# Two neighbouring chunks change places in every second channel tile of an RWKV-7 stage

## The chip, the cores and the metric

The kernel runs on one core of a Trainium2 chip. The core has a matrix engine (TensorE, in the profile PE, with its weight loads as PEld), VectorE (DVE), ScalarE (ACT), GpSimd (POOL), a queue engine (SP) and 16 DMA engines. Each engine takes its own instructions in order and waits for the others by semaphores. SBUF is the working memory with 128 partitions; PSUM receives what TensorE computes, in banks of 512 fp32 values a partition. The metric is the device time of one execution in microseconds, and lower is better.

## The reference

One decoder layer over 1024 tokens of 1024 channels. After an RMSNorm and one input projection, an RWKV-7 mixer of 8 heads of 64 channels and a sparse attention run in parallel; their outputs are gated, merged and projected, and a SwiGLU network and a last norm follow. The part that the change touches is the recurrence:

```python
def step(state, inp):
    r_t, d_t, k_t, v_t, kk_t, a_t = inp
    sa = jnp.einsum('bhij,bhj->bhi', state, -kk_t)
    state = (state * d_t[:, :, None, :] + sa[..., None] * (kk_t * a_t)[:, :, None, :]
             + v_t[..., None] * k_t[:, :, None, :])
    return state, jnp.einsum('bhij,bhj->bhi', state, r_t)
```

Then y is normalized for each head, scaled and shifted, a bonus is added and the sum is multiplied by a gate.

## The kernel before

**Halves, quarters, pairs, chunks.** The 1024 tokens are handled as two halves of 512. `rwkv(half, ...)` goes through two quarters of 256 tokens each (q = 0 to 3 over the whole run), a quarter has two pairs `pr`, a pair two chunks of 64 tokens, `pa` = 0 and 1. The 512 channels of the mixer are four channel tiles `ct` of 128 partitions, so two heads share a channel tile: head h is in tile h // 2, in its upper or lower 64 partitions.

**What comes ahead of a chunk.** The projections of the mixer (`proj_rwkv`, before the stage) write each channel tile with its 1024 tokens to DRAM, one DMA from a staging tile of which there are two (L307). A quarter loads its 256 tokens (L528), computes decays and gates (L547 to L566), norms (L593 to L612), the products of keys and queries for each chunk (L667, masked into MT at L671), their transposes (L686 into NAT), and inverts triangular 64x64 blocks: a chain of 62 small VectorE instructions (L705, L707) on 32x32 blocks, whose result goes through DRAM into TT (L709, L718), is transposed to TZ (L721), and is completed on TensorE (L735, L756).

**Positions.** In the tiles of a pair, chunk pa = 0 has its corrected values in partitions 64 to 127 (`ba` = 64 - 64 pa) and its plain values in 0 to 63 (`kb` = 64 pa); chunk pa = 1 the other way round. So TT, rhs and UV hold both chunks side by side in the partitions.

**A step of a chunk** is a chain across three engines (L783 to L817): matmuls of the state with AR (L788, eight heads); on VectorE, the result is added to `rhs` (L794), and on ScalarE the other half is copied to y2 (L795); eight matmuls with TT (L800), where all heads use the 64 rows and 64 output partitions at `ba`; a copy with a minus sign to UV (L802); eight matmuls with NAT (L810); and two VectorE instructions that make the new state (L813, L814). Behind each pair come the outputs of both chunks (L821), the inner products of the next pair (L745), and a norm. `finish` (L762) transposes, scales, adds the bonus and multiplies by the gate; that of the first pair stands in the last chunk's step.

**Filler.** The order on TensorE is written out by hand. `fill` is a queue of generators with matmuls of other stages: projections, attention of half 0, the merge and the first part of the feed-forward network. `pump(n)` emits about n matmuls of it at the place where it is called, in pieces that are mostly of four; `ticks(n, m)` emits n in m pieces, and steps the selection of the attention in between (`beside`). So each link of the chain has a number of filler matmuls behind it: in half 0 these are 6, 6 and 7, in half 1 they are 8, 8 and 9. Between the triangular inversion's start and L735 stand 251, 236, 281 and 241 in the four quarters. The order on the other engines is made by a scheduler from the program, with its own costs and priorities.

**Weights.** Filler tiles take weights of 512 KB through three staging buffers, split into two parts by L114 on ScalarE and L115 on VectorE; three products of the parts stand for one fp32 matmul (L140, L141, L145).

Of the kernel before, what the change touches and what calls it, by code (L numbers as in the profile page):

```python
# [18 lines left out]
AF = mybir.ActivationFunctionType  # L19
ALU = mybir.AluOpType  # L20
# [14 lines left out]
CT_R, CT_K, CT_V, CT_WA, CT_GD = 0, 4, 8, 12, 13  # L35
# [6 lines left out]
P_N1, P_N2, P_NF, P_MU, P_W0, P_A0, P_KK, P_KA, P_LG, P_LB, P_RK = 0, 8, 16, 24, 38, 42, 46, 50, 54, 58, 62  # L42
# [7 lines left out]
def block_kernel(ctx: ExitStack, tc: tile.TileContext, ins: dict, outT: bass.AP, stop=None, dbg=None):  # L50
    nc = tc.nc
    V, A, G, T, SY = nc.vector, nc.scalar, nc.gpsimd, nc.tensor, nc.sync
# [10 lines left out]
    par = cp.tile([128, NPAR], F32, name="par")  # L63
# [8 lines left out]
    hb = cp.tile([128, 16], F32, name="hb")  # L72
# [217 lines left out]
    def shifted(st, half, ct, x):  # L290
# [226 lines left out]
    def rwkv(half, p, consts, ready=None):  # L517
# [5 lines left out]
        for q in range(2 * half, 2 * half + 2):  # L523
# [17 lines left out]
            for c in range(2):  # L541
                pss = [mix(), mix()]
                for e in range(2):
                    ct = 2 * c + e
                    for i, ps in enumerate(pss):
                        half_ = slice(64 * i, 64 * i + 64)
                        T.matmul(ps[:, e * 256:(e + 1) * 256], wup[half_, ct * 128:(ct + 1) * 128], wa[half_, :],  # L547
                                 start=True, stop=True)
                for i, t in enumerate((L, ta)):
                    for ct in (2 * c, 2 * c + 1):  # L550
                        A.activation(t[:, ct, :], pss[i][:, ct % 2 * 256:ct % 2 * 256 + 256], AF.Tanh, scale=0.5,
                                     bias=hb[:, 4 * i + ct:4 * i + ct + 1])
# [6 lines left out]
            P = p.tile([128, 4, 4, 65], F32, tag="P", name="P")  # L559
# [27 lines left out]
            ps = sums(sq)  # L587
# [3 lines left out]
            ps = mix()  # L591
# [170 lines left out]
            def finish(pr, yc, y2):  # L762
                pt = mix()
                pg = mix()
                yT = y2.rearrange("p (c t) -> p c t", c=4)
                for ct in range(4):
                    T.transpose(pt[:, ct * 128:(ct + 1) * 128], yc[:, ct * 128:(ct + 1) * 128], ident)
                    T.matmul(pg[:, ct * 128:(ct + 1) * 128], gup[:, ct * 128:(ct + 1) * 128],
                             sg[:, pr * 128:(pr + 1) * 128], start=True, stop=True)
                for ct in range(4):  # L770
                    A.activation(yT[:, ct, :], pt[:, ct * 128:(ct + 1) * 128], AF.Identity,
                                 scale=par[:, P_LG + ct:P_LG + ct + 1], bias=par[:, P_LB + ct:P_LB + ct + 1])
# [6 lines left out]
            for pr in range(2):  # L779
                yb = p.tile([128, 2, 512], F32, tag=("P", "x6")[pr], name="yb")  # L780
                yc, y2 = yb[:, 0, :], yb[:, 1, :]
                for pa in range(2):
                    c = 2 * pr + pa  # L783
                    ba, kb = 64 - 64 * pa, 64 * pa
                    st = sref[0]
                    as_ = [mix(), mix()]
                    for h, ct, ro, hc in hd:
                        T.matmul(as_[h % 2][:, ct * 64:ct * 64 + 64],  # L788
                                 AR[ro, ct, c, :, :].rearrange("p s t -> p (s t)"), st[ro, ct, :],
                                 start=True, stop=True)  # L790
                    for g in range(2):
                        a4 = as_[g][:, 0:256].rearrange("p (c t) -> p c t", c=4)
                        r4 = rhs.rearrange("p (c g t) -> p c g t", c=4, g=2)[ba:ba + 64, :, g, :]
                        V.tensor_tensor(r4, a4[ba:ba + 64], r4, op=ALU.add)  # L794
                        A.activation(y2.rearrange("p (c g t) -> p c g t", c=4, g=2)[kb:kb + 64, :, g, :],  # L795
                                     a4[kb:kb + 64], AF.Copy)
                    pump(6 if half == 0 else 8)
                    ps = mix()
                    for h, ct, ro, hc in hd:
                        T.matmul(ps[ba:ba + 64, hc], TT[ba:ba + 64, pr, h, :], rhs[ba:ba + 64, hc],  # L800
                                 start=True, stop=True)
                    A.activation(UV[pr][ba:ba + 64, pa, :], ps[ba:ba + 64, :], AF.Copy, scale=-1.0)  # L802
                    if late and pa == 1:
                        finish(*late)
                        late = None
                    else:
                        pump(6 if half == 0 else 8)
                    ps = mix()
                    for h, ct, ro, hc in hd:
                        T.matmul(ps[ro, ct * 64:ct * 64 + 64], NAT[pr][:, pa, hc], UV[pr][:, pa, hc],  # L810
                                 start=True, stop=True)
                    new = cp.tile([128, 4, 64], F32, tag="S", name="S", bufs=2)
                    V.tensor_tensor(new, ps[:, 0:256].rearrange("p (c t) -> p c t", c=4), st, op=ALU.add)  # L813
                    V.tensor_tensor(new, new, PC[:, :, c:c + 1].to_broadcast([128, 4, 64]), op=ALU.mult)  # L814
# [677 lines left out]
```

## Time and profile before

| | |
|---|---|
| runs | 1746.47, 1748.87, 1750.44 us (median 1748.87) |
| profiled execution | 1748.71 us |
| its span, first to last instruction | 1746.9 us |
| TensorE busy | 1708.1 us (98%) |
| VectorE busy | 1114.3 us (64%) |
| ScalarE busy | 833.3 us (48%) |
| DMA | 247.14 MB, mean 141 GB/s |

The profile has a page with busy times, a span cut into slices, DMA queues, the chain that ended last, and the costliest groups of instructions. Further views list groups by line and form, the instructions in order of time, waits, and busy times of given stretches. A group's row reads: line, engine, operation, output<-inputs, rows*columns of the array and shape, count | busy us, mean ns of one | idle time before it, and what ended that. In the order of time, a row begins with start and duration in us from the span's start. A matmul in fp32 is two passes, and each pass has a record of its own; the end of a pass is modelled.

### The profile page before, as it was taken

Reading aid. Unit: us, or ns where it says so; the run is one execution under the profiler, and the core shown is the slowest. Engines: PE = TensorE matmul, PEld = TensorE weight load, DVE = VectorE, ACT = ScalarE, POOL = GpSimd, SP = SyncE. Lnnn points to the kernel's source line nnn. Section 1 sums busy time; section 2 is a strip of 40 time slices with the busy share of each in tenths; the row PEclk is TensorE's granted clock in tenths of the full one; section 3 lists DMA queues with packets and bytes.
Section 4 is the critical chain, followed back from the end, with each engine's and each line's share of the span. In section 5 each row is a group of like instructions: output and inputs, shape, how many; then the busy total and the mean of one; then the engine's idle time right before and its main releaser. Section 6 shows DMA issues by size and latency. Waiting matters only on the chain.

```text
span 1746.9 us, 26692 instructions
## 1 busy us (share of the span) xinstructions
PE 1708.1 (98%) x10156; PEld 1410.3 (81%) x10156; DVE 1114.3 (64%) x2133; ACT 833.3 (48%) x1547; POOL 100.5 (6%) x123
## 2 busy tenths in 40 slices
PE   8999999999999998999999999999999999999997
PEld 6888888778878776878787888888788888888887
DVE  6789899857468567857876655445465564454464
ACT  6365998453445687645333455433234322232241
POOL 0000000010021111000100321000000000000000
PEclk9999999999999999999999999999999999999999
DMA  5542224536357535644343765173464344434442
GB/s 210 173 138 94 97 97 145 163 97 171 100 178 201 149 121 157 197 146 118 97 127 93 234 165 138 61 225 113 165 213 140 109 136 151 136 96 150 139 124 93
DMA packets 132383, 247.14 MB, mean 141 GB/s; under 512 B 36848, under 2 KB 60080, under 8 KB 132128
## 3 DMA queue, kind: packets, MB, share of 16 engines
q1 hardware_dynamic: 108896, 171.61, 31.7%
q10 hardware_dynamic: 15552, 47.75, 8.7%
q0 software_dynamic: 7808, 26.09, 5.6%
q8 instruction: 80, 1.31, 0.3%
q14 instruction: 47, 0.39, 0.1%
HBM read 192.40 MB, written 53.00 MB: 140 GB/s over the span
## 4 chain that ended last, share of the span: by engine, by line
PE 50%; issue 1%; DVE 1%; ACT 0%; POOLq 0%; POOL 0%; DVEq 0%; ACTq 0%
PE acc L145 14%; PE acc L140 13%; PE acc L141 13%; PE acc L156 3%; PE mix L1053 1%; PE mix L1029 1%; PE mix L1043 1%; PE acc L1197 0%; PE mix L800 0%; PE mix L788 0%; PE acc L1201 0%; ACT whi L114 0%; DVE h L1272 0%; PE mix L254 0%; PE mix L810 0%
## 5 line engine op out<-in xcount | busy, mean ns | idle before, releaser
L115 DVE TENSOR_TENSOR wlo<-wst,whi 128x1024 fp32r<-128x1024 f32 (+1 forms) x229 | 277.5, 1214 | 276.0 <-PE acc L145 132.7
L114 ACT ACTIVATE whi<-wst 128x1024 fp32r<-128x1024 f32 (+1 forms) x229 | 238.3, 1043 | 262.7 <-PE acc L141 186.9
L140 PE MATMUL acc<-zhi,whi 128*128 128x512 f32 x672 | 264.8, 394 | 0.0
L141 PE MATMUL acc<-zlo,whi 128*128 128x512 f32 x672 | 262.0, 390 | 0.0
L145 PE MATMUL acc<-zhi,wlo 128*128 128x512 f32 x672 | 170.2, 392 | 0.0
L140 PEld LDWEIGHTS acc<-zhi,whi 128*128 128x128 f32 x672 | 126.2, 188 | 26.8 <-issue 1.9
L141 PEld LDWEIGHTS acc<-zlo,whi 128*128 128x128 f32 x672 | 126.3, 188 | 24.8
L145 PEld LDWEIGHTS acc<-zhi,wlo 128*128 128x128 f32 x672 | 124.8, 188 | 25.4 <-issue 0.7
L140 PE MATMUL acc<-u1hi,whi 128*128 128x512 f32 x352 | 140.5, 399 | 0.1
L141 PE MATMUL acc<-u1lo,whi 128*128 128x512 f32 x352 | 137.6, 391 | 0.0
L140 PE MATMUL acc<-u0hi,whi 128*128 128x512 f32 (+1 forms) x352 | 135.5, 387 | 1.7 <-DVE tmp L323 1.7
L141 PE MATMUL acc<-u0lo,whi 128*128 128x512 f32 (+1 forms) x352 | 133.8, 383 | 0.0
L140 PE MATMUL acc<-fhi,whi 128*128 128x512 f32 (+1 forms) x318 | 114.3, 368 | 2.3 <-ACT whi L114 1.5
L141 PE MATMUL acc<-flo,whi 128*128 128x512 f32 (+1 forms) x318 | 112.9, 364 | 0.2 <-DVE flo L115 0.2
L145 PE MATMUL acc<-u1hi,wlo 128*128 128x512 f32 x352 | 90.0, 394 | 0.0
L145 PE MATMUL acc<-u0hi,wlo 128*128 128x512 f32 (+1 forms) x352 | 85.7, 384 | 0.0
L114 ACT ACTIVATE fhi<-tmp 128x512 fp32r<-128x512 f32 x44 | 27.7, 630 | 112.6 <-DVE tmp L1229 112.3
L140 PEld LDWEIGHTS acc<-u0hi,whi 128*128 128x128 f32 x352 | 66.2, 188 | 14.9 <-ACT stg L114 2.1
L140 PEld LDWEIGHTS acc<-u1hi,whi 128*128 128x128 f32 x352 | 66.2, 188 | 14.8 <-issue 1.3
L141 PEld LDWEIGHTS acc<-u1lo,whi 128*128 128x128 f32 x352 | 66.2, 188 | 12.6
L141 PEld LDWEIGHTS acc<-u0lo,whi 128*128 128x128 f32 x352 | 66.2, 188 | 12.1
L145 PEld LDWEIGHTS acc<-u1hi,wlo 128*128 128x128 f32 x352 | 64.9, 188 | 13.7 <-issue 0.9
(328 smaller groups left out, 3204.2 us busy)
## 6 DMA issues: line engine op xcount, KB each, us to landing
wst<-in_w_ffn_in SPq DMA_DIRECT2D x72, 512.0 KB, 3.6
wst<-in_w_in ACTq DMA_DIRECT2D x36, 512.0 KB, 4.5
wst<-in_w_in SPq DMA_DIRECT2D x27, 512.0 KB, 4.0
wst<-in_w_fo SPq DMA_DIRECT2D x25, 512.0 KB, 3.8
k<-d_k POOLq DMA_DIRECT2D x24, 512.0 KB, 7.9
h<-in_xT SPq DMA_DIRECT2D x32, 256.0 KB, 5.2
d_g<-tmp ACTq DMA_DIRECT2D x32, 256.0 KB, 3.4
tmp<-d_g SPq DMA_DIRECT2D x32, 256.0 KB, 3.7
```

Source lines behind the costliest of these rows:

```text
L114: A.activation(hi, x, AF.Copy)
L115: V.tensor_tensor(lo, x, hi.bitcast(F32), op=ALU.subtract)
L140: T.matmul(ps, whi[:, wk + k, :], ahi[:, ak + k, tok], start=k == 0, stop=False)
L141: T.matmul(ps, whi[:, wk + k, :], alo[:, ak + k, tok], start=False, stop=False)
L145: T.matmul(ps, wlo[:, wk + k, :], ahi[:, ak + k, tok], start=False, stop=k == nk - 1)
L156: T.matmul(ps, w[:, k, :], a[:, k, tok], start=k == 0 and w is whi and a is ahi, stop=k == nk - 1 and a is alo)
L1029: T.matmul(ps[:, :w], q[bi // 2][:, e, bi % 2 * 128:bi % 2 * 128 + 128], k[:, i, e, c:c + w], start=i == 0, stop=i == 1)
L1043: T.transpose(ps[:, j * 128:(j + 1) * 128], L[:, (c + j) * 128:(c + j + 1) * 128], ident)
L1053: T.matmul(py[64 * e:64 * e + 64, bi * 128:(bi + 1) * 128], v[:, j, 64 * e:64 * e + 64], pts[e][j // 4][:, j % 4, :], start=j == b, stop=j ...
```

## The change

In odd channel tiles the two chunks of each pair change places. The swap is made on the way: where the projections of r, k and v write odd channel tiles to DRAM, two DMAs with pieces of 64 tokens write each pair's two chunks into each other's place; the tanh of decay and gate inputs writes odd tiles in two pieces; the decays at the chunks' ends (PC) are copied in three instructions. In a step, `at[x]` gives for even (x = 0) and odd (x = 1) channel tiles the position and the partitions of the chunk in hand, and the instructions over all four tiles become one for even and one for odd tiles: four adds and four copies for two and two, two copies to UV for one. The TT matmuls go through the heads in the order 0, 2, 1, 3, 4, 6, 5, 7, and take their partitions by tile. `finish` swaps back, with two ScalarE instructions for each odd tile and three adds for one.

With it, the filler behind the links of a step is 8, 8 and 9 matmuls in both halves, and that ahead of L735 in quarter 0 is 211.

```diff
+    def swapped(x):
+        return x.rearrange("p (n s t) -> p n s t", s=2, t=64)
...
-                SY.dma_start(d_rw[g0][j], st.rearrange("p h t -> p (h t)"))
+                if g0 in (CT_R, CT_K, CT_V) and j % 2:
+                    d, t = (swapped(x) for x in (d_rw[g0][j], st.rearrange("p h t -> p (h t)")))
+                    for i in range(2):
+                        SY.dma_start(d[:, :, i, :], t[:, :, 1 - i, :])
+                else:
+                    SY.dma_start(d_rw[g0][j], st.rearrange("p h t -> p (h t)"))
...
+                        xy = [(x, y)] if ct % 2 == 0 else [(swapped(x)[:, :, j, :], swapped(y)[:, :, 1 - j, :])
+                                                           for j in range(2)]
...
-            V.tensor_copy(PC, P[:, :, :, 64])
+            V.tensor_copy(PC[:, 0::2, :], P[:, 0::2, :, 64])
+            for i in range(2):
+                V.tensor_copy(PC[:, 1::2, i::2], P[:, 1::2, 1 - i::2, 64])
...
-            ticks((251, 236, 281, 241)[q], (13, 4, 10, 6)[q])
+            ticks((211, 236, 281, 241)[q], (13, 4, 10, 6)[q])
...
-                V.tensor_tensor(yT, yT, bon[:, :, pr * 128:(pr + 1) * 128], op=ALU.add)
+                b = bon[:, :, pr * 128:(pr + 1) * 128]
+                V.tensor_tensor(yT[:, 0::2, :], yT[:, 0::2, :], b[:, 0::2, :], op=ALU.add)
+                for i in range(2):
+                    y = yT[:, 1::2, 64 * i:64 * i + 64]
+                    V.tensor_tensor(y, y, b[:, 1::2, 64 - 64 * i:128 - 64 * i], op=ALU.add)
...
-                    ba, kb = 64 - 64 * pa, 64 * pa
+                    at = [(pa ^ x, 64 - 64 * (pa ^ x), 64 * (pa ^ x)) for x in range(2)]
...
-                        r4 = rhs.rearrange("p (c g t) -> p c g t", c=4, g=2)[ba:ba + 64, :, g, :]
-                        V.tensor_tensor(r4, a4[ba:ba + 64], r4, op=ALU.add)
-                        A.activation(y2.rearrange("p (c g t) -> p c g t", c=4, g=2)[kb:kb + 64, :, g, :],
-                                     a4[kb:kb + 64], AF.Copy)
-                    pump(6 if half == 0 else 8)
+                        for x, (pp, ba, kb) in enumerate(at):
+                            r4 = rhs.rearrange("p (c g t) -> p c g t", c=4, g=2)[ba:ba + 64, x::2, g, :]
+                            V.tensor_tensor(r4, tiles(x, as_[g][ba:ba + 64, 0:256]), r4, op=ALU.add)
+                    for g in range(2):
+                        for x, (pp, ba, kb) in enumerate(at):
+                            A.activation(y2.rearrange("p (c g t) -> p c g t", c=4, g=2)[kb:kb + 64, x::2, g, :],
+                                         tiles(x, as_[g][kb:kb + 64, 0:256]), AF.Copy)
+                    pump(8)
                     ps = mix()
-                    for h, ct, ro, hc in hd:
+                    for h, ct, ro, hc in (hd[i] for i in (0, 2, 1, 3, 4, 6, 5, 7)):
+                        ba = at[ct % 2][1]
                         T.matmul(ps[ba:ba + 64, hc], TT[ba:ba + 64, pr, h, :], rhs[ba:ba + 64, hc],
                                  start=True, stop=True)
-                    A.activation(UV[pr][ba:ba + 64, pa, :], ps[ba:ba + 64, :], AF.Copy, scale=-1.0)
+                    for x, (pp, ba, kb) in enumerate(at):
+                        A.activation(tiles(x, UV[pr][ba:ba + 64, pp, :]), tiles(x, ps[ba:ba + 64, :]), AF.Copy, scale=-1.0)
...
-                        pump(6 if half == 0 else 8)
+                        pump(8)
...
-                        pump(7 if half == 0 else 9)
+                        pump(9)
```

More of the change, by code (lines that the diff above doesn't have):

```diff
@@ L770, in finish @@
                 for ct in range(4):
-                    A.activation(yT[:, ct, :], pt[:, ct * 128:(ct + 1) * 128], AF.Identity,
-                                 scale=par[:, P_LG + ct:P_LG + ct + 1], bias=par[:, P_LB + ct:P_LB + ct + 1])
-                V.tensor_tensor(yT, yT, bon[:, :, pr * 128:(pr + 1) * 128], op=ALU.add)
+                    x, y = pt[:, ct * 128:(ct + 1) * 128], yT[:, ct, :]
+                    xy = [(x, y)] if ct % 2 == 0 else [(x[:, 64 - 64 * i:128 - 64 * i], y[:, 64 * i:64 * i + 64])
+                                                       for i in range(2)]
+                    for x, y in xy:
+                        A.activation(y, x, AF.Identity, scale=par[:, P_LG + ct:P_LG + ct + 1],
+                                     bias=par[:, P_LB + ct:P_LB + ct + 1])
+                b = bon[:, :, pr * 128:(pr + 1) * 128]
[3 more added lines that the diff above has]
+                    V.tensor_tensor(y, y, b[:, 1::2, 64 - 64 * i:128 - 64 * i], op=ALU.add)
                 V.tensor_tensor(yT, yT, pg.rearrange("p (c t) -> p c t", c=4), op=ALU.mult)
@@ L806, in rwkv @@
                     else:
-                        pump(6 if half == 0 else 8)
+                        pump(8)
                     ps = mix()
                     for h, ct, ro, hc in hd:
-                        T.matmul(ps[ro, ct * 64:ct * 64 + 64], NAT[pr][:, pa, hc], UV[pr][:, pa, hc],
+                        pp = at[ct % 2][0]
+                        T.matmul(ps[ro, ct * 64:ct * 64 + 64], NAT[pr][:, pp, hc], UV[pr][:, pp, hc],
                                  start=True, stop=True)
```

10 lines of the change are left out of this document (6 added, 4 removed).

## The prediction

> **What bounds the kernel now.** First the page: busy times, then stretches of time, then groups by form.
>
> ```profile
> PE 1708.1 (98%) x10156; PEld 1410.3 (81%) x10156; DVE 1114.3 (64%) x2133; ACT 833.3 (48%) x1547; POOL 100.5 (6%) x123
> ...
> 350.00:393.00 43.00, 41.01 (x264) 32.93 (x263) 25.46 (x46) 22.51 (x53) 4.52 (x2) 1.00 0.38 99
> 393.00:437.00 44.00, 44.00 (x198) 36.49 (x198) 30.97 (x81) 16.03 (x28) 0.77 (x1) 1.00 0.60 172
> 480.00:620.00 140.00, 137.13 (x1099) 109.86 (x1097) 93.45 (x225) 79.35 (x171) 26.14 (x32) 1.00 0.60 176
> 620.00:800.00 180.00, 171.00 (x1335) 136.97 (x1334) 123.14 (x257) 124.41 (x271) 10.55 (x6) 0.98 0.49 150
> 800.00:960.00 160.00, 156.25 (x1142) 127.19 (x1141) 118.37 (x226) 59.75 (x98) 10.09 (x5) 1.00 0.37 110
> ```
>
> A row of stretches reads: stretch, length, then busy time and count of PE, PEld, DVE, ACT, POOL, granted clock, DMA share, GB/s. The RWKV stage (the first to the last of its lines) lies between about 345 and 955 us, and even there PE is busy for 95% or more: every wait is covered by filler matmuls of other stages. The total of filler is fixed, so the time is the sum of what TensorE issues plus the few gaps. An edit is worth what it takes off that sum, unless it opens a gap. (A busy row is modelled with a tail, so I work below with distances from start to start.) The groups by form, RWKV lines only:
>
> ```profile
> L800 PE MATMUL mix<-rhs,TT 64*64 64x64 f32 x256 | 18.3, 222 | 0.0
> L788 PE MATMUL mix<-S,AR 64*128 64x64 f32 x256 | 17.7, 278 | 0.3 <-DVE S L814 0.3
> L745 PE MATMUL mix<-UV,MT 64*64 64x64 f32 x256 | 9.2, 221 | 0.0
> L821 PE MATMUL mix<-UV,MT 128*64 128x64 f32 x256 | 8.8, 222 | 0.0
> ```
>
> L800 and L745 have the same shape and number (64 rows, 64 columns, 64 wide, x256, two passes for each fp32 matmul), yet L800 takes twice the time. The order of time shows how. One chunk of quarter 2, then the last chunk:
>
> ```profile
> 769.06 0.75 DVE L794 TENSOR_TENSOR rhs<-mix,rhs 64x256 f32<-64x256 f32 x2 [0.60 <-PE mix L788]
> 771.00 1.14 PE L800 MATMUL mix<-rhs,TT 64*64 64x64 f32 x16
> 771.28 0.65 ACT L795 ACTIVATE yb<-mix 64x256 f32<-64x256 f32 x2
> 772.08 1.19 PE L145 MATMUL acc<-mhi,wlo 128*128 128x512 f32 x4
> 772.18 0.59 ACT L802 ACTIVATE UV<-mix 64x512 f32<-64x512 f32 x1 [0.25 <-PE mix L800]
> 774.12 0.69 PE L810 MATMUL mix<-UV,NAT 128*64 128x64 f32 x16
> 775.11 0.42 DVE L813 TENSOR_TENSOR S<-mix,S 128x256 f32<-128x256 f32 x1
> 775.67 1.15 PE L745 MATMUL mix<-UV,MT 64*64 64x64 f32 x32
> 775.91 0.69 DVE L828 TENSOR_TENSOR yb<-mix,yb 128x512 f32<-128x512 f32 x1
> 776.75 1.11 PE L788 MATMUL mix<-S,AR 64*128 64x64 f32 x16
> ...
> 946.80 1.14 PE L800 MATMUL mix<-rhs,TT 64*64 64x64 f32 x16
> 947.87 0.33 PE L767 MATMUL mix<-kc,yb 128*128 128x128 f32 x1
> ```
>
> L800 holds TensorE 772.08 - 771.00 = 1.08 us (1.07 in the last chunk) for 16 passes: 67 ns each. L745 takes 776.75 - 775.67 = 1.08 us for 32 passes: 34 ns each. L745 goes through the list `both`, so neighbours in its order use opposite 64-row, 64-column corners of the array; in L800 all eight heads of a chunk use the same corner, `ba`.
>
> **The change, part by part.**
>
> *Corners of L800 alternate.* Odd channel tiles now hold the chunk's neighbour, so in one step the heads of even tiles are at `ba` and those of odd tiles at 64 - `ba`, and the new head order 0, 2, 1, 3, 4, 6, 5, 7 alternates them: the pattern of L745. Bounds: nothing (67 ns stays, L800 itself), or the 34 ns of L745; no row of this shape is faster. I take 34 ns, as L745 equals it in shape, data type and alternation: 16 chunks x (1.07 - 0.54) = 8.5 us off the sum. L788, L810 and L821 keep their shapes, heads and column halves: 0.
>
> The Trainium skill speaks against this. TensorEngine Tiling (Array Packing), section Restrictions and Gotchas, says that different row tiles cannot access one PSUM bank at the same time; both corners of the new L800 write one bank, and by that rule the sum here would be 0 and not 8.5. L745 writes both corners into one bank as well, at 34 ns, so the trace disagrees.
>
> *More VectorE and ScalarE instructions in each chunk.* Prices: 0.42 us for 256 elements a partition (L813), 0.69 for 512 (L828), so 0.27 per 256, and half a 64x256 add (0.75 / 2 = 0.38) is 0.24. The adds become four: 0.96 for 0.75, +0.2. The copies to y2 become four: 0.20 each for 0.65 together, +0.15. The copy to UV becomes two of about 0.33: +0.1. They lie in the links L788 -> add -> L800 -> UV -> L810. In the chunk shown the adds end at 769.81 and L800 starts at 771.00 (1.19 us to spare); the UV copy ends at 772.77 and L810 starts at 774.12 (1.35). The growth fits: cost 0 where the cover is 8 filler matmuls. Without that cover each link pays its own growth, 0.45 a chunk, 7 us in all.
>
> *Covers of half 0 grow from 6, 6, 7 to 8, 8, 9 matmuls, and those ahead of L735 in quarter 0 fall from 251 to 211.* That is 18 more for each of quarters 0 and 1 and 40 fewer: filler moves, and the four left run later. A filler matmul comes every 0.227 us:
>
> ```profile
> 1158.66 1.81 PE acc L145 x8
> 1164.10 1.81 PE acc L145 x8
> ```
>
> (24 of them in 5.44 us.) So quarter 0 loses 40 x 0.227 = 9.1 us of cover over the triangular solve, whose end is the transposes to TZ that L735 reads:
>
> ```profile
> 418.82 0.17 DVE L707 TENSOR_TENSOR W<-W,tw 128x16 f32<-128x16 f32 x1
> 429.70 0.88 DVE L721 STREAM_TRANSPOSE TZ<-TT 32x256 f32<-32x256 f32 x2
> 442.49 1.20 PE L735 MATMUL mix<-TZ,MT 32*32 32x32 f32 x64
> ```
>
> TZ is ready at 430.58, 11.9 us before L735 starts; 2.8 us stay. Cost 0; behind that, 1 us per us.
>
> *Shifts by whole pairs of filler.* From the order of the built kernel: in quarter 1 four more filler matmuls come ahead of L593, and in quarter 2 L735 has 268 behind the stage before it instead of 272. Rows of both places:
>
> ```profile
> 512.27 0.41 PE L593 MATMUL mix<-kc,nq 128*128 128x128 f32 x2 [1.18 <-DVE nq L589]
> ...
> 754.09 0.69 PE L735 MATMUL mix<-TZ,MT 32*32 32x32 f32 x30 [0.16 <-DVE TZ L721]
> ```
>
> The first wait shrinks by 4 x 0.227 = 0.9, the second, which just waits already, grows by 0.9. Sum 0.
>
> *Queue order on ScalarE in quarter 1*, where attention shares the steps. In the built order an eviction L1045 and an exponential L1034 now stand ahead of the two UV copies, where before they stood behind, and in one step a pass of the selection, L944, too:
>
> ```profile
> 605.61 0.62 ACT L1034 ACTIVATE L<-L,mx 128x384 f32<-128x384 f32 x1
> 606.13 0.18 ACT L1034 ACTIVATION_READ_ACCUMULATOR L<-L,mx 128x1 f32 x1
> 606.33 0.38 ACT L1045 ACTIVATE pt<-mix 128x256 f32<-128x256 f32 x1
> 607.07 0.59 ACT L802 ACTIVATE UV<-mix 64x512 f32<-64x512 f32 x1 [0.18 <-PE mix L800]
> 607.94 1.14 ACT L944 ACTIVATE junkl<-kept,z 128x1024 int8<-128x1024 f32 x1
> 608.11 0.55 PEld L810 LDWEIGHTS mix<-UV,NAT 128*64 128x64 f32 x16 [0.37 <-ACT ge L952]
> ```
>
> From the end of L800: 0.38 + 0.62 + 0.18 for the accumulator read + 0.66 for UV = 1.84 us, against a cover of 8 x 0.227 = 1.82. Between 0 (they run under L800) and 1.1 us a step (L944 is added) for four steps: 0 to 4.5 us. I take 1.5, nearer to the lower end, as part of that queue runs before L800 ends.
>
> *The rest.* Each quarter: 12 tanh for 8, three copies for one into PC; each `finish`: two more ScalarE instructions and three adds for one (0.42 + 2 x 0.29 for 0.69). They stand among filler, with DVE at 64% and ACT at 48%: 0. Six staged tiles go out in two DMAs of 256-byte pieces:
>
> ```profile
> d_rw<-stg SPq DMA_DIRECT2D x14, 512.0 KB, 4.3
> d_w<-W SPq DMA_DIRECT2D x8, 128.0 KB, 5.7
> ```
>
> The nearest row with small pieces, d_w in pieces of 128 bytes, lands in 5.7 us against 4.3. A projection tile takes 48 x 0.227 = 10.9 us and there are two staging buffers, so a few us more hold up neither the buffer nor, on SP's queue, the weight loads that are three buffers ahead: 0. If that cover were gone, 12 DMAs x 5.7 us would be the price.
>
> **Sum** against the profiled execution (1748.71 us, span 1746.9, within 0.2 us of the median 1748.87): -8.5 - 0.9 + 0.9 + 1.5 = -7.0, so 1741.7 us.
>
> **Rivals.**
>
> *The corners don't overlap (the change doesn't do what it says).* Then only the 1.5 us of ScalarE's queue stays: 1750.2. For it: L788 alternates its 64-row halves and still takes 65 ns a pass, so alternation alone is not enough. Against it: L788 has 128 columns, and L745, with 64, runs at 34. Chance 0.06. By the Trainium skill's rule on banks (TensorEngine Tiling, above) this is what would happen.
>
> *Quarter 0's solve becomes the bound.* From the last W step to the last transpose it takes 430.58 - 418.99 = 11.6 us in quarter 0, but in quarter 1:
>
> ```profile
> 571.22 0.19 DVE L707 TENSOR_TENSOR W<-W,tw 128x16 f32<-128x16 f32 x1
> ...
> 586.10 0.90 DVE L721 STREAM_TRANSPOSE TZ<-TT 32x256 f32<-32x256 f32 x2 [1.42 <-DMA TT<-d_w]
> ```
>
> 15.6 us, 4.0 longer. If the same befell quarter 0, L735 would wait 4.0 - 2.8 = 1.2 us: 1742.9. It spoils the gain only from 2.8 + 7.0 us on. Chance 0.10, still faster.
>
> *The links become the bound: slower.* 16 chunks have three links each (adds, UV, state), 48 in all. If the longer instruction chains overrun their cover by 0.15 us a link, the gain is gone; from 0.22 us on (10.5 / 48) the kernel is slower by over 3.5 us; at 0.25 it is 1740.2 + 12.0 = 1752.2 with the queue term inside it. For it: half 1 keeps its covers of 8, 8, 9 while its chains grow by 0.45 us a chunk. Against it: the 1.19 and 1.35 us to spare above. Chance 0.07, and 0.12 that the overrun is 0.1 to 0.2 us, which leaves about 1747.
>
> **How the numbers follow.** Forecast 0.65 (its own range 1737 to 1745), the solve 0.10, a partial overrun 0.12, no overlap 0.06, links 0.07. Besides these, gaps can gain or lose a halved clock:
>
> ```profile
> 680.00:690.00 10.00, 6.24 (x36) 4.98 (x37) 8.56 (x15) 7.05 (x15) 0.00 (x0) 0.83 0.66 186
> ```
>
> Here TensorE idles and the granted clock falls to 0.83 over 10 us, 1.7 us lost; one such stretch more or less widens the range by 1.7 each way, and the queue's 0 to 4.5 us is inside. So low is 1740.2 - 0.9 - 1.7 = 1737.6, put at 1736.5 for a slightly smaller L800; high is 1747.5, which takes in most of the partial overrun and leaves out no overlap and links. About 0.2% (3.5 us) is what a measurement of this kernel can tell: faster takes the forecast, the solve and a little of the overrun, 0.77; same most of the overrun and part of no overlap, 0.15; slower 0.08.
>
> **What would show it.** The group of L800 at about 9.2 us busy for 256 passes, and 0.54 us from its start to what follows: right; 18 us: the first rival. L735 in quarter 0 without a wait for TZ. Idle time ahead of L810 and L800 in the list of waits: under 2 us in all if the covers hold, 7 us or more if the links bind. DMA queues and the projection stage before 345 us unchanged. What would make the prediction wrong is a gap in half 1, above all ahead of L810, or a changed queue order in quarter 2, where TensorE already idles.

## The result, and the profile after

| | before | after |
|---|---|---|
| median of 4 runs | 1748.07 us (1746.47 to 1750.44) | 1739.55 us (1737.58 to 1741.15) |
| profiled execution | 1748.71 us | 1741.15 us |
| its span | 1746.9 us | 1739.4 us |

The ratio is 0.9941, with a 95% interval of 0.9925 to 0.9957: the kernel became 0.6% faster. Between the profiled executions lie 7.6 us, where the prediction had 7.0.

In the changed kernel the line numbers are higher: L788 became L812 (state), L794 L822 (adds), L795 L825 (copies), L800 L831 (TT), L802 L834 (UV), L810 L843 (NAT), L735 L750, L721 L736, L593 L608, L745 L760. The page of the changed kernel gives the busy times, and the groups by form give the matmuls of a step:

```profile
PE 1706.6 (98%) x10156; PEld 1407.9 (81%) x10156; DVE 1123.0 (65%) x2189; ACT 846.9 (49%) x1627; POOL 98.5 (6%) x123
```

```profile
L812 PE MATMUL mix<-S,AR 64*128 64x64 f32 x256 | 18.7, 285 | 0.4 <-DVE S L847 0.2
L831 PE MATMUL mix<-rhs,TT 64*64 64x64 f32 x256 | 11.8, 231 | 0.6 <-DVE mx L1064 0.5
L843 PE MATMUL mix<-UV,NAT 128*64 128x64 f32 x256 | 11.2, 229 | 0.8 <-ACT UV L834 0.7
L760 PE MATMUL mix<-UV,MT 64*64 64x64 f32 x256 | 9.2, 221 | 0.0
```

The number of matmuls is the same. The TT group fell from 18.3 to 11.8 us busy; L760 kept its 9.2, which the prediction gave L831 as well. The order of time of the changed kernel shows one step of quarter 1:

```profile
621.58 0.68 PE L831 MATMUL mix<-rhs,TT 64*64 64x64 f32 x16
622.19 0.33 PE L782 MATMUL mix<-kc,yb 128*128 128x128 f32 x1
622.20 1.14 ACT L977 ACTIVATE junkl<-kept,z 128x1024 int8<-128x1024 f32 x1
...
623.34 0.71 ACT L1067 ACTIVATE L<-L,mx 128x512 f32<-128x512 f32 x1
623.95 0.19 ACT L1067 ACTIVATION_READ_ACCUMULATOR L<-L,mx 128x1 f32 x1
624.04 0.77 ACT L834 ACTIVATE UV<-mix 64x256 f32<-64x256 f32 x2
624.46 0.97 PE L843 MATMUL mix<-UV,NAT 128*64 128x64 f32 x16 [0.72 <-ACT UV L834]
```

Sixteen passes hold TensorE for 622.19 - 621.58 = 0.61 us, against 1.07. In the trace 12 of the 16 groups take 0.61; the other four take 0.72 to 1.08, one of them in a stretch of halved clock. The second thing to see is the queue of ScalarE: the two UV copies stand behind L977 and L1067 (1.14 and 0.71 us, with an accumulator read of 0.19), and L843 waits 0.72 us for them.

The list of waits of TensorE for the RWKV stage, 345 to 960 us, before:

```profile
PE mix L593 <- DVE nq L589: 2.6, 2, 1.5
PE mix L612 <- ACT nrT L606: 2.4, 2, 1.7
PE mix L686 <- ACT NAT L689: 2.2, 1, 2.2
```

and after (waited in total, times, longest):

```profile
PE mix L701 <- DVE MT L686: 3.3, 1, 3.3
PE mix L682 <- DVE MT L686: 2.1, 3, 0.8
PE mix L608 <- DVE nq L604: 1.0, 2, 0.9
...
PE mix L843 <- ACT UV L834: 0.7, 1, 0.7
...
PE mix L831 <- DVE mx L1064: 0.5, 1, 0.5
```

All rows of the list together make 17.4 us before and 11.1 after. Hardly any of it belongs to the chunks' links; the norms and masks ahead of the chunks (L593 to L701) wait most, before and after. The saving on these waits was not in the prediction.

Part of it is given back by the granted clock. In the two traces it stands at 0.5 within the stage for two stretches of 3.4 us before, and for two of 6.8 us after (590.1 and 682.2). Ten microseconds around each, after (stretch, length, busy time and count of PE, PEld, DVE, ACT, POOL, granted clock, DMA share, GB/s):

```profile
588.00:598.00 10.00, 9.83 (x110) 7.81 (x110) 1.59 (x6) 8.65 (x21) 1.20 (x2) 0.66 0.10 29
680.00:690.00 10.00, 6.48 (x37) 5.93 (x38) 7.85 (x14) 7.78 (x20) 0.00 (x0) 0.66 0.55 142
```

**An account of the span.** I set up one for the profiled execution of every kernel. Waits are those of TensorE in the stage (the sum of the rows); the cost of the halved clock is estimated as half of the length of its stretches there. "Start" and "end" are measured between the traces, matmul by matmul: start is how much later than before the last projection matmuls ahead of the stage begin, and end is how much of the difference arises behind the stage, from the L140 at 1541.88 us of before to the last instruction. "Rest" is the span's difference from before, less start, less end, and less the differences of waits and halved clock. "Place" is how many more filler matmuls than in the kernel before have been issued by the end of half 0, from the numbers in the code.

| kernel | swap | place | span us | start | waits | halved clock | end | rest |
|---|---|---|---|---|---|---|---|---|
| before | no | 0 | 1746.9 | 0 | 17.4 | 3.4 | 0 | 0 |
| e1_covers | no | -4 | 1748.1 | +2.3 | 11.9 | 6.8 | +0.4 | +0.6 |
| e2_split | no | -4 | 1747.3 | +2.0 | 10.1 | 8.5 | +0.1 | +0.5 |
| after | yes | -4 | 1739.4 | +2.2 | 11.1 | 6.8 | +0.6 | -7.4 |
| e4_order | yes | -4 | 1736.7 | +0.8 | 11.4 | 3.4 | +0.6 | -5.6 |
| e5_after_again | yes | -4 | 1741.8 | +1.4 | 14.1 | 5.1 | +0.6 | -5.6 |
| e6_banks | yes | -4 | 1740.0 | +0.3 | 15.2 | 3.4 | +0.6 | -5.6 |
| e7_ready | yes | -4 | 1744.4 | +1.7 | 15.2 | 5.1 | +0.6 | -4.2 |
| e3_oldcovers | yes | 0 | 1746.8 | +1.8 | 20.2 | 5.1 | +0.2 | -6.6 |
| e12_t215 | yes | 0 | 1744.0 | +1.4 | 15.4 | 8.5 | +0.1 | -7.5 |
| e11_t229 | yes | +14 | 1744.6 | +1.2 | 21.3 | 3.4 | +0.1 | -7.5 |
| e9_links_only | yes | +36 | 1760.3 | +2.0 | 28.4 | 13.7 | +0.1 | -9.9 |
| e10_ticks_only | yes | -40 | 1762.0 | +1.5 | 28.0 | 15.4 | +0.6 | -9.5 |
| e8_ticks | yes | -44 | 1767.4 | +1.9 | 31.3 | 20.5 | +0.2 | -12.6 |

The start is the time until TensorE runs at full speed. In the trace of after the first matmuls stay slow for longer; rows of the order of time, after and then before:

```profile
12.32 0.63 PE L394 MATMUL acc<-u0hi,whi 128*128 128x512 f32 x1
12.75 0.63 PE L395 MATMUL acc<-u0lo,whi 128*128 128x512 f32 x1
```

```profile
11.59 0.39 PE L384 MATMUL acc<-u0hi,whi 128*128 128x512 f32 x1
11.82 0.39 PE L385 MATMUL acc<-u0lo,whi 128*128 128x512 f32 x1
```

They come every 0.43 us after and every 0.23 us before; in the traces' own record of the granted clock, 1.0 begins at 16.6 and at 10.1 us. At the end of the projection stage the L145 that starts at 341.03 us before starts at 343.22 after: 2.2 us, before any step of the stage has run. At the end of the span the granted clock falls to 0.5 once more, 9.2 us ahead of the last instruction after and 6.2 before.

With these taken out, the rest is +0.5 and +0.6 in the two kernels without the swap, and -4.2 to -7.5 in the eight with it whose place is near. In e8, e9 and e10 it is larger, as their waits partly lie within halved stretches and so count twice. The overlap is in the rest. The account does not tell more than about 2 us: the changed kernel itself gives -7.4 in one execution and -5.6 in another, and e7's -4.2 is not explained.

### The profile page after: what moved, and what is told of

It is laid out like the page before. It is cut to its first block, busy times and chain, and to the rows that moved or that the text cites. A ratio compares the mean times of both kernels' runs of the same rounds, so it can differ in the third digit from the quotient of the medians.

```text
span 1739.4 us, 26865 instructions
## 1 busy us (share of the span) xinstructions
PE 1706.6 (98%) x10156; PEld 1407.9 (81%) x10156; DVE 1123.0 (65%) x2189; ACT 846.9 (49%) x1627; POOL 98.5 (6%) x123
## 4 chain that ended last, share of the span: by engine, by line
PE 78%; DVE 9%; ACT 6%; issue 3%; DMA 3%; POOL 0%; SPq 0%; ACTq 0%; DVEq 0%; POOLq 0%
PE acc L140 20%; PE acc L145 19%; PE acc L141 19%; PE acc L156 3%; PE mix L1086 2%; PE mix L1062 2%; PE mix L1076 2%; ACT junk L977 2%; DVE wlo L115 1%; ACT junkl L977 1%; PE mix L927 1%; DVE junk L974 1%; DMA wst<-in_w_ffn_in 1%; ACT whi L114 1%; PE acc L1230 1%
## 5 line engine op out<-in xcount | busy, mean ns | idle before, releaser
L140 PE MATMUL acc<-zhi,whi 128*128 128x512 f32 x672 | 264.7, 394 | 0.0
L145 PE MATMUL acc<-zhi,wlo 128*128 128x512 f32 x672 | 170.2, 392 | 0.0
L140 PEld LDWEIGHTS acc<-zhi,whi 128*128 128x128 f32 x672 | 126.2, 188 | 26.9 <-issue 1.7
L145 PEld LDWEIGHTS acc<-zhi,wlo 128*128 128x128 f32 x672 | 124.7, 188 | 25.5 <-issue 0.7
L140 PE MATMUL acc<-u1hi,whi 128*128 128x512 f32 x352 | 141.0, 401 | 0.1
L140 PE MATMUL acc<-u0hi,whi 128*128 128x512 f32 (+1 forms) x352 | 135.3, 387 | 1.8 <-DVE tmp L333 1.8
L140 PE MATMUL acc<-fhi,whi 128*128 128x512 f32 (+1 forms) x318 | 114.0, 367 | 2.0 <-ACT whi L114 1.0
L145 PE MATMUL acc<-u1hi,wlo 128*128 128x512 f32 x352 | 90.5, 397 | 0.0
L145 PE MATMUL acc<-u0hi,wlo 128*128 128x512 f32 (+1 forms) x352 | 86.5, 385 | 0.0
L140 PEld LDWEIGHTS acc<-u0hi,whi 128*128 128x128 f32 x352 | 66.2, 188 | 15.3 <-ACT stg L114 2.2
L140 PEld LDWEIGHTS acc<-u1hi,whi 128*128 128x128 f32 x352 | 66.4, 189 | 14.4 <-issue 0.9
L145 PEld LDWEIGHTS acc<-u1hi,wlo 128*128 128x128 f32 x352 | 65.5, 190 | 14.0 <-issue 0.9
L141 PEld LDWEIGHTS acc<-u1lo,whi 128*128 128x128 f32 x352 | 66.5, 189 | 12.6
```

Of the source, the lines that this page charges most:

```text
L140: T.matmul(ps, whi[:, wk + k, :], ahi[:, ak + k, tok], start=k == 0, stop=False)
L141: T.matmul(ps, whi[:, wk + k, :], alo[:, ak + k, tok], start=False, stop=False)
L145: T.matmul(ps, wlo[:, wk + k, :], ahi[:, ak + k, tok], start=False, stop=k == nk - 1)
```

## The experiments

The theory: the overlap of the corners is the gain, the longer links are hidden by the 8, 8 and 9 filler matmuls, and the moved filler in itself is worth nothing. The rivals: the gain comes from the moved filler; two banks or the order of the heads matter; the links or quarter 0's solve are close to binding.

**The moved filler alone.** The kernel before, with the filler numbers of the change (the 8 and 9 of half 1 now in both halves, and 211):

```diff
-            ticks((251, 236, 281, 241)[q], (13, 4, 10, 6)[q])
+            ticks((211, 236, 281, 241)[q], (13, 4, 10, 6)[q])
...
-                    pump(6 if half == 0 else 8)
+                    pump(8)
...
-                        pump(7 if half == 0 else 9)
+                        pump(9)
```

> The kernel before with the changed kernel's numbers of filler matmuls alone (8, 8, 9 behind the links of half 0, 211 ahead of the completion of the inverse in quarter 0); no tile is swapped. Theory (the gain is the overlap of TT matmuls in opposite corners): the TT groups stay at 1.07 us for 16 passes, and the time is within 2 us of before (1746 to 1750). Rival (the moved filler closes gaps, and that is the gain): 1739 to 1743, with the TT groups still at 1.07.

Measured: 1752.75 us against 1751.32, ratio 0.9997 (0.9977 to 1.0017). The group by form:

```profile
L800 PE MATMUL mix<-rhs,TT 64*64 64x64 f32 x256 | 18.5, 221 | 0.7 <-DVE rhs L794 0.7
```

The group is as before, and so is the time. By the account the moved filler did take 5.5 us off the waits; 3.4 of halved clock and 2.3 of start stand against it in the profiled execution. The medians show no gain, and by the interval it can be 4 us at most.

**The instructions split, without the swap.** The same, with the adds, y2 copies and UV copies split by even and odd tiles, at the old positions:

```diff
...
+                        for x in range(2):
+                            r4 = rhs.rearrange("p (c g t) -> p c g t", c=4, g=2)[ba:ba + 64, x::2, g, :]
+                            V.tensor_tensor(r4, tiles(x, as_[g][ba:ba + 64, 0:256]), r4, op=ALU.add)
...
+                    for x in range(2):
+                        A.activation(tiles(x, UV[pr][ba:ba + 64, pa, :]), tiles(x, ps[ba:ba + 64, :]), AF.Copy, scale=-1.0)
```

> As the run with the covers alone, and the instructions of a step split as in the changed kernel (four adds, four copies, two copies to UV), both parts at the same position, so all TT matmuls stay in one corner. Theory: the split costs 0 to 2 us over the covers alone, 1746 to 1752. Rival (the longer instruction chains overrun their covers and hide a larger gain): 5 us or more over the covers alone, with idle time ahead of the TT and NAT matmuls.

Measured: 1747.55 against 1751.32, ratio 0.9976 (0.9961 to 0.9991).

```profile
L805 PE MATMUL mix<-rhs,TT 64*64 64x64 f32 x256 | 18.5, 223 | 0.1
```

The TT group still takes 18.5 us, and no link overruns (0.1 us idle ahead of it). So the longer links cost nothing behind these covers. But this kernel, without the swap, is itself faster than before, by 0.24%, and clear of 1; the covers alone were not. Some 4 us of the change's gain may thus not be the swap's. What is left between this kernel and the changed one, 0.9976 against 0.9941 (or 0.9951 when the changed kernel ran again, below), is 0.25 to 0.35%, or 4 to 6 us; the interval of the second run overlaps this one, so the size is loose, and the stronger evidence is the group's 0.61 us in the traces. It fits the rest in the account and the shape of the group: 16 x (1.07 - 0.61) = 7.4 us less some lost to waits within the steps.

**The swap with the old covers.** The changed kernel with 6, 6, 7 in half 0, and 251:

> The changed kernel with the old numbers of filler matmuls (6, 6, 7 in half 0, and 251 ahead of the completion of the inverse in quarter 0). Theory: the TT groups keep their 0.61 us, and only half 0 pays for its shorter covers, at most 0.45 us for each of 8 chunks: 1739 to 1744. Rival (the moved filler is the gain): 1746 to 1750.

Measured: 1749.50 against 1751.32, ratio 0.9984 (0.9975 to 0.9994). The group, then a chunk of half 0 in order of time:

```profile
L831 PE MATMUL mix<-rhs,TT 64*64 64x64 f32 x256 | 12.8, 227 | 0.7 <-DVE rhs L822 0.7
```

```profile
474.89 1.25 DVE L822 TENSOR_TENSOR rhs<-mix,rhs 64x128 f32<-64x128 f32 x4 [1.26 <-PE mix L812]
475.59 1.19 ACT L825 ACTIVATE yb<-mix 64x128 f32<-64x128 f32 x4 [1.63 <-DVE rhs L822]
...
475.95 0.80 PE L831 MATMUL mix<-rhs,TT 64*64 64x64 f32 x16
476.79 0.78 ACT L834 ACTIVATE UV<-mix 64x256 f32<-64x256 f32 x2
```

Here TensorE comes to the TT group before the adds are done: L831 starts at 475.95, while the last of the four adds ends at 474.89 + 1.25 = 476.14, and the group is stretched to 0.80, against 0.68 where nothing waits. The rows also give the prices of the split instructions: four adds take 1.25 us, four copies 1.19 and two UV copies 0.78. The theory's 1739 to 1744 missed, and the time is in the rival's range, although the rival's reason, the moved filler by itself, fell in e1. So the new numbers are needed for the gain to come through: with the old ones it is 0.16%, with the new ones 0.59% (0.49% when run again, below). Little of that difference is in the links. The TT group is busy 1.0 us longer and waits 0.7 us, against 0.6; the waits of the stage are 20.2 us here against 11.1, and the largest of them stand ahead of L608, L701 and L619, outside the chunks.

**The order of the heads.** The changed kernel with `for h, ct, ro, hc in hd:` in the TT loop, so that the heads come as 0 to 7 and the two heads of a tile, four passes, use one corner before the next tile uses the other:

> The changed kernel with the TT matmuls in the order of the heads, 0 to 7, so that two neighbouring heads of a channel tile share a corner and the corner changes after every second head. Theory (neighbours in opposite corners overlap, neighbours in one corner do not): about 0.8 us for 16 passes, between 0.61 and 1.07, and 2 to 4 us over the changed kernel, 1741 to 1744. Rival (it is enough that a group uses both corners, as TensorE takes what is free): 0.61 us and 1739 to 1741.

Measured: 1744.10 against 1751.32, ratio 0.9960 (0.9946 to 0.9975). Group and order of time:

```profile
L831 PE MATMUL mix<-rhs,TT 64*64 64x64 f32 x256 | 12.0, 227 | 0.6 <-DVE mx L1064 0.5
```

```profile
440.83 0.73 PE L831 MATMUL mix<-rhs,TT 64*64 64x64 f32 x16
441.49 0.73 PE L145 MATMUL acc<-u0hi,wlo 128*128 128x512 f32 x2
```

The group takes 441.49 - 440.83 = 0.66 us instead of 0.61: 0.8 us over all 16 chunks. That is nearer to the rival than to the theory's 0.8. That both corners are used in one group brings nearly all of the overlap; strict alternation adds the last 0.05 of 0.46 us.

**Two banks, and the changed kernel again.** One kernel is the changed one unedited; in the other even and odd tiles write to a PSUM bank each:

```diff
-                    ps = mix()
+                    ps2 = [mix(), mix()]
...
-                        T.matmul(ps[ba:ba + 64, hc], TT[ba:ba + 64, pr, h, :], rhs[ba:ba + 64, hc],
+                        T.matmul(ps2[ct % 2][ba:ba + 64, hc], TT[ba:ba + 64, pr, h, :], rhs[ba:ba + 64, hc],
...
```

> The changed kernel once more, on the chip of the next three, as their base and for its gaps. Theory: 1737 to 1742, TT groups at 0.61 us for 16 passes where nothing waits; the stretches with a halved clock at the start and in quarter 1 differ from the first profile if they are chance, and recur if the order of the work makes them.

> The changed kernel with the TT matmuls of the two corners writing into two PSUM banks instead of one. Rule of the Trainium skill (TensorEngine Tiling (Array Packing), Restrictions and Gotchas: different row tiles cannot use one bank at the same time): the group gets shorter than the 0.61 us that it takes in one bank, and the time falls by up to 5 us. Theory (the corners overlap in one bank as in two): 0.61 us in both, and the time within 2 us of the changed kernel.

Measured, on one chip: unedited 1742.51 against 1751.78, ratio 0.9951 (0.9930 to 0.9972), half a microsecond above the expected range; two banks 1741.45, ratio 0.9934 (0.9909 to 0.9959). With two banks:

```profile
442.08 0.68 PE L831 MATMUL mix<-rhs,TT 64*64 64x64 f32 x16
442.69 1.19 PE L145 MATMUL acc<-u0hi,wlo 128*128 128x512 f32 x4
```

Again 0.61 us. The rule of the Trainium skill (TensorEngine Tiling (Array Packing), Restrictions and Gotchas) that different row tiles cannot access one PSUM bank at the same time does not show for these 64x64 corners: one bank and two take the same time. The second run of the changed kernel also shows how much of a profile is chance. Its halved stretches are at 442, 596 and 688, 3.4 us each, where the first had 590 and 682, 6.8 us each: two come again in about the same place, at half the length, and one is new.

**An attempt on the largest wait left.** In quarter 2 the call of `ready()`, which ends the FFN's first tile, was moved from ahead of the MT loop to behind the NAT loop:

```diff
-            if q == 2:
-                ready()
...
+            if q == 2:
+                ready()
```

> The changed kernel with the opening of the merge in quarter 2 (the call of ready, with the split of the attention and mixer outputs of half 0) moved from ahead of the key-query products to behind their transposes. Theory on the gap there (TensorE waits 3.3 us and more because VectorE splits eight merge tiles among the masks, and the idle stretch halves the clock for 6.8 us): the waits ahead of the transposes in quarter 2 fall from 5 us to under 1.5 and the halved clock goes, 3 to 6 us less than the changed kernel, 1734 to 1737. Rival (the splits only move into the triangular inverse's chain, which is already the last to arrive in quarter 2): the wait reappears ahead of the completion of the inverse, and the time stays within 2 us.

Measured: 1745.86 against 1751.78, ratio 0.9967 (0.9952 to 0.9981), some 3 us slower than the unedited one by the medians, with intervals that overlap. The hoped-for 1734 to 1737 missed. The waits for MT in quarter 2 fell, from 4.8 us in after to 1.3, and the work that was moved became late in its turn:

```profile
700.54 0.50 PE L140 MATMUL acc<-yhi,whi 128*128 128x512 f32 x1 [3.16 <-DVE tmp L1190]
```

One wait of 3.3 us went and one of 3.2 came, though not ahead of the inverse, where the rival had it.

**Less filler ahead of quarter 0's L750.** The changed kernel with 171 for 211, to take away the 2.7 us that the solve has left:

> The changed kernel with another 40 filler matmuls (9.1 us) taken from the stretch ahead of the completion of the inverse in quarter 0, 171 instead of 211. Theory (the inverse is ready 2.7 us before it is used there, and what is taken beyond that is a wait at 1 us per us): a wait of 6 us or so ahead of these matmuls in quarter 0 and 1744 to 1748. Rival (the scheduler or the attention further on takes the wait back, as the filler only moves): 1738 to 1742.

Measured: 1766.72 against 1751.78, ratio 1.0084 (1.0051 to 1.0117). Both expectations missed this. Five rows in order of time, and one stretch:

```profile
427.53 0.22 PE L750 MATMUL mix<-TZ,MT 32*32 32x32 f32 x2 [3.15 <-DVE TZ L736]
...
541.86 0.52 SPq L538 DMA_DIRECT2D wa<-d_rw  x1
...
548.47 0.42 ACT L549 ACTIVATE wa<-wa 64x256 f32<-64x256 f32 x1 [6.35 <-DMA wa<-d_rw]
549.74 0.39 ACT L1067 ACTIVATE L<-L,mx 128x128 f32<-128x128 f32 x1
...
550.27 0.48 PE L1076 MATMUL mix<-kc,L 128*128 128x128 f32 x1 [7.59 <-ACT L L1067]
```

```profile
427.00:445.00 18.00, 17.09 (x229) 13.66 (x229) 4.67 (x10) 6.07 (x16) 0.00 (x0) 0.62 0.30 82
```

L750 waits 3.15 us for TZ, as the solve's rival has it, and behind it the clock is halved for 13.7 us, though TensorE is busy for 17.09 of the 18. That costs 6.8 us by the estimate above, twice the wait. In quarter 1, with 44 filler matmuls fewer issued than before, the load of `wa` goes out on SP at 541.86 (at 535.96 in after) and lands 6.6 us later. ScalarE comes to it just behind its issue and stands for 6.35 us at L549; the attention's exponentials L1067 are queued behind it, and TensorE waits 7.59 us for these. One wait on a DMA has become a wait of two engines. Why the load goes out later here was not followed up.

**Which place of the filler.** Four more kernels, all with the swap. One has 8, 8, 9 with 251 (e9), one 6, 6, 7 with 211 (e10); the others are the changed kernel with 229 (e11) and 215 (e12) for 211.

> The changed kernel with the old 251 filler matmuls ahead of the completion of the inverse in quarter 0, and the new 8, 8, 9 behind the links of half 0; so the filler runs 40 further ahead from there on. Theory (the links of half 0 need the longer covers, and where the filler stands otherwise is of little weight): 1738 to 1743. Rival (what the old covers lost was the place at which the pieces of filler and of attention fall later, not the links): 1744 to 1750, as with the old covers.

> The changed kernel with the new 211 filler matmuls ahead of the completion of the inverse and the old 6, 6, 7 behind the links of half 0; the filler then runs 36 behind at the end of half 0. Theory (the links pay): TT groups with waits in half 0, 1743 to 1748. Rival (the place of the attention decides: 40 fewer matmuls ahead of it brought 24 us in the run with 171): 1750 or more, with idle time ahead of attention and norm matmuls in quarters 1 and 2.

> The changed kernel with 229 filler matmuls ahead of the completion of the inverse in quarter 0 instead of 211, so that at the end of quarter 0 the filler stands within 4 matmuls of the kernel before. Theory (little hangs on the place): within 3 us of the changed kernel, 1738 to 1744. Rival (the place decides): over 4 us away from it, to either side.

> The changed kernel with 215 filler matmuls ahead of the completion of the inverse in quarter 0 instead of 211: the filler then stands at the end of half 0 where it stood in the kernel before (18 + 18 - 36 = 0; the changed kernel is 4 behind, the slow runs are 36 ahead or 40 to 44 behind). Theory (the place at the end of half 0, where attention meets the opening of quarter 2, sets the loss): within 4 us of the changed kernel, 1738 to 1744 on a chip with the kernel before at 1748 to 1752. Rival (single pieces of four decide, not the distance): over 5 us away from it.

| kernel | place | median us | before, same chip | ratio (95%) |
|---|---|---|---|---|
| e9_links_only | +36 | 1762.59 | 1752.04 | 1.0065 (1.0046 to 1.0083) |
| e10_ticks_only | -40 | 1765.21 | 1752.04 | 1.0076 (1.0059 to 1.0093) |
| e11_t229 | +14 | 1746.51 | 1752.04 | 0.9971 (0.9959 to 0.9983) |
| e12_t215 | 0 | 1747.57 | 1749.96 | 0.9990 (0.9979 to 1.0001) |

The lists of waits for the stage, e9, then e10:

```profile
PE mix L627 <- ACT nrT L621: 4.4, 2, 2.4
PE mix L619 <- DVE nr L115: 3.6, 4, 1.6
PE mix L1076 <- ACT L L1067: 3.5, 1, 3.5
```

```profile
PE mix L1076 <- DVE mx L1064: 5.4, 1, 5.4
PE mix L627 <- ACT nrT L621: 4.0, 2, 2.0
...
PE mix L831 <- DVE rhs L822: 2.2, 2, 1.8
```

e9 missed both of its expectations; e10 and e12 came as their rivals had it. e11 lies above the theory's range, but its interval overlaps that of the changed kernel, so it decides nothing. In e9 and e10, the norms (L619, L627) and the attention (L1076) wait, and only 1.2 and 2.7 us stand ahead of L831; the links together (L812, L831, L843) wait 5.2 and 5.6 us of some 28. The TT group overlaps in both (11.9 us busy, and 13.3 in e10, where groups wait in their middle). So a kernel with the swap can be 0.8% slower than before by the place of its filler alone. In e12 only four filler matmuls (0.9 us of work) stand elsewhere than in the changed kernel, and of a gain of 0.49 to 0.59% there are 0.10% left. Its list for the stage:

```profile
PE mix L619 <- DVE nr L115: 3.5, 3, 1.7
PE mix L682 <- DVE MT L686: 3.2, 4, 1.1
```

These are waits for VectorE ahead of the chunks of quarters 1 to 3; in the trace of e12 the masks of MT (L686) in quarter 3 stand behind three VectorE instructions of the feed-forward network (L1260 to L1262, 0.69 us each), where in after the first mask comes ahead of the third. The four matmuls have changed what VectorE has in its queue at that moment. Why the place -4 is a good one, other than that the runs say so, was not found; nor was the kernel without the swap run at other places than 0 and -4.

## Why the prediction was right, point by point

The forecast was 1741.7 us and the chance of faster 0.77; the median came at 1739.55, and the profiled execution's difference at -7.6 for -7.0. Sign and size are right; the terms are right in part, and the sum is helped by terms that cancel.

- **Corners of L800 alternate: the mechanism right, the size 1.1 us too large.** 0.61 us a group, not 0.54: -7.4 instead of -8.5. With the four longer groups, all 16 together hold TensorE for 11.0 us from their first pass to the next matmul, against 17.2 before: 6.3 us came through. I halved the time a pass from L745, as if a group had no ends. L760 takes 1.08 us for 32 passes and L831 0.61 for 16; that is (1.08 - 0.61) / 16 = 29 ns a pass and about 0.14 us for the ends, which a short group pays in full.
- **"L788 alternates its 64-row halves and still takes 65 ns a pass": misread.** The single pass records of the trace tell it: those of L812 (and of L788 before) start in pairs, 7 ns apart, with 105 ns to the next pair; those of L831 in pairs 6 to 7 ns apart, with 52 ns to the next; those of L800 one by one, 58 ns apart. So the row halves of L812 do overlap; with twice the columns, a pair takes twice the time. The reading cost nothing, as that rival had a chance of 0.06, but it was no argument for it. That rival, and the rule of one bank behind it, fell in e6.
- **More instructions in each chunk: cost right, price wrong.** Four adds take 1.25 us and not 0.96, four copies 1.19 and not 0.80, two UV copies 0.78 and not 0.66: 1.2 us a chunk more than before, not 0.45. I had taken some 0.13 us off an instruction for half of its elements, from the rows of L813 and L828; a halved add came only 0.06 us cheaper (0.38 to 0.31) and a halved copy 0.03 (0.33 to 0.30). The 1.19 and 1.35 us to spare were enough for each link's part of it, as e2 shows (nothing lost), and with the old covers they were not (e3).
- **Covers moved: right as a sum, as far as the runs can tell.** e1 gives 0.9997, but e2, with the same covers, 0.9976, so up to 4 us may have come from here. And it is no rule that moved filler is worth nothing: at other places it made the kernel up to 15 us slower than before, gain included (e8 to e10). The step "filler moves, cost 0" held for the numbers chosen here, and for a reason that the prediction didn't give.
- **Quarter 0's solve: right.** Order of time after, VectorE and TensorE:

```profile
430.08 0.90 DVE L736 STREAM_TRANSPOSE TZ<-TT 32x256 f32<-32x256 f32 x2
```

```profile
433.15 0.39 PE L140 MATMUL acc<-u0hi,whi 128*128 128x512 f32 x1
...
433.70 0.98 PE L750 MATMUL mix<-TZ,MT 32*32 32x32 f32 x50
```

  TZ ends at 430.98, and L750 comes at 433.70 without a wait: 2.7 us to spare where 2.8 were predicted. "Behind that, 1 us per us" is wrong, too low: in e8 the 3.15 us of wait was followed by a halved clock that costs about 6.8 us.
- **Shifts by whole pairs: small, and not as predicted.** The wait at L608 in quarter 1 fell from 1.18 to 0.86 us, a third of the 0.9 forecast, and that of L750 in quarter 2 (0.16, forecast to grow by 0.9) is gone. Sum about -0.5 for 0.
- **Queue order on ScalarE: the mechanism right, the size half.** 0.72 us ahead of L843 in one of the four steps, behind L977 and L1067, for the 1.5 forecast. The 0.5 us ahead of L831 are no part of it: their releaser is L1064 on VectorE.
- **DMA halves: right.** From 33 us to the end of the projection stage the distance between the two traces stays at 2.2 us. The DMA groups of after say that the smaller transfers land sooner, not later as the row of d_w had suggested (that row itself, unchanged by the edit, went from 5.7 to 4.0):

```profile
d_rw<-stg SPq DMA_DIRECT2D x8, 512.0 KB, 3.4
d_rw<-stg SPq DMA_DIRECT2D x12, 256.0 KB, 2.7
```

- **Left out: the waits of the whole stage.** They fell by 6.3 us, the cost of the halved clock in it grew by 3.4 us, the start by 2.2 and the end by 0.6. With -7.4 for the group that makes -7.4 - 6.3 + 3.4 + 2.2 + 0.6 = -7.5, as the spans have it; that it closes so well is chance, by the account's 2 us. The prediction treated the waits ahead of L593 to L701 as fixed; the runs show the stage's waits between 10 and 31 us, by the place of the filler. The range held since these terms happened to cancel, not since it had allowed for them. The closeness of -7.6 to -7.0 is luck, and the sign held at this place of the filler, not at every one.

## What to carry to other kernels

Small fp32 matmuls that all use one corner of the array can be made to overlap by giving half of them the opposite corner; what it saves is read from a group with that alternation in the same trace, but a group of 16 passes also pays its ends. In a kernel with a hand-ordered filler, try the filler's place by a few matmuls together with the change: here four of them took most of its gain. Compare the sum of the waits and the stretches of halved clock beside the time, so that a gain of the change and a gain of the place can be told apart.

## What the runs showed of the hardware that was not expected

- Two passes in opposite 64x64 corners start 6 to 7 ns apart, with the same PSUM bank or with two (0.61 us a group in both). In the order 0 to 7 the group takes 0.66 us and its passes still start in pairs, 13 or 4 ns apart and then 45 or 54, though four in a row use one corner.
- The granted clock fell to 0.5 for 3.4 to 13.7 us at a time, and stayed there with TensorE busy again (17.09 of 18 us in e8). A long wait stood ahead of the stretch in e8, but not of every one: ahead of the stretch at 590 us of after, the list has TensorE waiting 0.4 and 0.2 us, at L771, among 32x32 matmuls. By half of their length those stretches cost between 3.4 and 20.5 us in a profiled execution, and they are longer where the waits are: 3.4 to 8.5 with waits of 10 to 21 us in all, 13.7 to 20.5 with 28 to 31.
- At the start the granted clock reached 1.0 anywhere between 10 and 17 us, and the matmuls behind the start stood up to 2.3 us later than in before.
- Here a VectorE instruction of half the size took far more than half the time: two 64x256 adds take 0.75 us, four 64x128 adds 1.25, so 0.38 and 0.31 each.
